# A hybrid encoder layer on one core: the first norm and the five begun weight pairs written out in a fixed order, TensorE kept turning the identity while it waits for x, the set-up vectors loaded later, and a weight pair begun after each tile of the two later norms

## The chip, the cores and the metric

The kernel runs on one core of one Trainium2 chip. The metric is the device time of one execution in microseconds (us). All times in this document are of that kind unless a sentence says otherwise. The engines carry the names of the profile: PE is TensorE's matrix multiplication and PEld its weight load, DVE is VectorE, ACT is ScalarE, POOL is GpSimd, SP is SyncE. ACTq, SPq and POOLq are the same engines where they issue a DMA transfer. "L113" is line 113 of the kernel before; the changed kernel has numbers of its own from its line 343 on.

## What is computed

One layer on x of 1024 rows by 1024 columns, all in float32:

```
x = x + 0.5 * swiglu_ffn(rms_norm(x, ffn1_norm), ffn1_w_in, ffn1_w_out)
u = rms_norm(x, mix_norm)
q_a,k_a,v_a, q_b,k_b,v_b, gate_logits = split(u @ w_mix_in)
y_a = chunked_band_attention(q_a, k_a, v_a, rel_bias_a)
lam = exp(sum(lambda_q1*lambda_k1)) - exp(sum(lambda_q2*lambda_k2)) + 0.2
y_b = rms_norm(diff_attention(q_b, k_b, v_b, t5_bias, lam), subln_g) * 0.8
g_a, g_b = split(sigmoid(gate_logits + b_gate))
x = x + (g_a*(y_a @ w_branch_a) + g_b*(y_b @ w_branch_b)) @ w_o
x = x + 0.5 * swiglu_ffn(rms_norm(x, ffn2_norm), ffn2_w_in, ffn2_w_out)
out = rms_norm(x, final_norm)
```

`swiglu_ffn` multiplies by a 1024 x 5632 matrix, takes silu(gate) * up and multiplies by a 2816 x 1024 matrix. Three small inputs return below as "the set-up vectors": the four lambda vectors of 64 numbers, `subln_g` of 128 and `b_gate` of 2048.

## The kernel before, in words

**A product in three pieces.** Every large float32 multiplication is made of three single-pass ones. Each operand is split into a high part, which an ACT cast rounds off (`whi` of a weight, `A11h` and the like of an activation, L97), and a low part, which DVE subtracts (`wlo`, `A11l`, L102). Then PE adds hi·hi, lo·hi and hi·lo (`mm3`, L128 to L130). "A product" below is one such PE instruction of 128x512.

**A pair in seven.** The multiplications by `ffn1_w_in` are made in Strassen-Winograd form. A pair is one block of 128 gate columns and the block of 128 up columns that goes with it. It needs seven block products, A11·B11, S1·T1, A12·B21, S2·T2, S4·B22, S3·T3 and A22·N4, of 12 PE products each. A11, A12, A22 and the sums S1 to S4 come from the normed and transposed x, and the B's and their differences T1 to T3 and N4 from the raw weights, which arrive in two transfers of 512 KB. PSUM has six banks for products ("mm") and two for transposes ("tr"). A pair holds three of the six in turn (its chains q, r and s). ACT copies a finished chain to SBUF (`c<-prod`, L287) or DVE adds the next one to it (`c<-prod,c`, L113), and only then is the bank free again.

**Begun pairs.** A11·B11 and A12·B21 need only the upper four row tiles and the first weight block. So five pairs are begun early (`head`, L343 to L348): these two block products are made, their sum is passed through silu and stored to a DRAM buffer (`gb`), and the other five are made later (`rest`, L350). The mixer's input projection begins seven pairs in the same way.

**Norms.** x has eight row tiles of 128. Each tile is loaded (`xt`), squared and summed on ACT (`junk`, L174), given its inverse root on POOL (`r<-v`, L139), scaled by DVE (L181) and transposed by PE in two halves of four (`tr`, L208). `norm0` (L214) makes A11 and A12 from tiles 0 to 3, `norm1a` S1 from tiles 4 to 7, `norm1b` S2 and S4, and `norm1c` S3 and A22. The opening (L657 to L688) does this for the first norm and calls the begun pairs between. `renorm` (L545) does it for the two later norms, behind `ffn1_w_out` (the mixer's norm) and behind `w_o`. There the rows are called `xc`, and `late` (L564) runs norm1a for its four tiles and then begins the remaining pairs by L571: `for _ in range(4 + extra_heads): next(projection, None)`.

**Set-up.** `setup` (L601) is a generator with four stages. Its first stage loads the set-up vectors on POOL's queue (`lv` L614, `gsub` L620, `bg_rows` L623), takes the dot products of the lambdas on DVE (L617) and transposes the gate bias (`trb`, L625). The later stages write the two relative-bias tables to DRAM. `ffn_in` calls it at pairs 5, 8, 11 and 14, each time behind the latest silu (`issue_after`). The exponentials of the two dot products (`le`, L776 and L777) stand in the text where attention begins.

**What sets the order.** Each engine runs its instructions in one fixed order, and an instruction that waits holds all behind it on its engine. A scheduler of the framework orders the program when it is built. It places each instruction by its own estimates of time, so that an instruction may run far from where its line stands. The names in the listings below have a number behind them that tells one buffer from the next.

## Time and profile before

| what | value |
|---|---|
| time, median of 3 runs | 2115.16 us (2114.83 to 2117.82) |
| time of the profiled execution | 2114.65 us |
| its span on the chip | 2112.9 us |
| mean granted TensorE clock | 0.993 |
| PE busy | 2045.6 us, 97% of the span, 9901 instructions |
| DVE busy | 1379.1 us, 65% |
| ACT busy | 955.5 us, 45% |
| POOL busy | 142.8 us, 7% |

The times of the views below are microseconds from the start of the span. The time of an execution is 1.75 us more than its span here (2114.65 less 2112.9). In a timeline a row reads: start, duration, engine, line, operation, output<-inputs, how many, and in brackets how long the engine was idle before it and what ended that. A row for several instructions runs to the end of the last. The end of a matmul in the trace is modelled, so the step from one start to the next is what tells its price.

### The profile page before, as it was taken

To read this page: it belongs to the slowest core of one execution; us is meant where nothing else is said; L and a number is where in the kernel's file an instruction comes from. 1 tells how busy PE (TensorE), PEld (TensorE's weight loads), DVE (VectorE), ACT (ScalarE), POOL (GpSimd) and SP (SyncE) were. 2 spreads that over 40 slices of the span, in tenths; PEclk is the share of its full clock that TensorE was granted. 3 is DMA by queue.
4 is the path that set the end of the run, shared out by engine and by line. 5 is a ranking of instruction groups with operands and counts; after the bars stand their busy time and mean duration, and the time that the engine had idled before them with its cause. 6 is when DMAs were issued, how large, how long until landed. Compare 5 with 4: busy or idle time off the path is not lost.

```text
span 2112.9 us, 28240 instructions
## 1 busy us (share of the span) xinstructions
PE 2045.6 (97%) x9901; PEld 1700.4 (80%) x9901; DVE 1379.1 (65%) x2459; ACT 955.5 (45%) x1825; POOL 142.8 (7%) x202
## 2 busy tenths in 40 slices
PE   6899999999999999999999999999899999999997
PEld 4688888888888788899877888787788888888886
DVE  6765656658567856654657787668766666668566
ACT  6433333334446644433467666157433333334444
POOL 2300000000001000000046211000000000000001
PEclk9999999999999999999999999999999999999999
DMA  5743323376344644743495365644542333275334
GB/s 166 213 135 100 125 86 104 105 261 214 99 135 143 195 135 130 234 145 115 158 302 178 111 221 167 229 139 127 163 144 91 125 96 107 92 278 201 99 116 160
DMA packets 272996, 324.61 MB, mean 154 GB/s; under 512 B 15070, under 2 KB 167662, under 8 KB 272852
## 3 DMA queue, kind: packets, MB, share of 16 engines
q1 hardware_dynamic: 271664, 319.55, 46.2%
q0 software_dynamic: 1184, 3.24, 0.6%
q8 instruction: 78, 1.28, 0.2%
q14 instruction: 66, 0.54, 0.1%
q10 hardware_dynamic: 4, 0.00, 0.0%
HBM read 221.74 MB, written 100.99 MB: 153 GB/s over the span
## 4 chain that ended last, share of the span: by engine, by line
PE 86%; DVE 6%; issue 3%; ACT 2%; DMA 2%; POOL 0%; SPq 0%; ACTq 0%; DVEq 0%; POOLq 0%
PE prod L128 19%; PE prod L129 19%; PE prod L130 18%; PE po L129 7%; PE po L128 7%; PE po L130 7%; PE pt L822 2%; DVE wlo L102 2%; PE pv L906 1%; PE pb L128 1%; PE pb L129 1%; PE pb L130 1%; PE sc L806 1%; PE sc L807 1%; PE pv L970 1%
## 5 line engine op out<-in xcount | busy, mean ns | idle before, releaser
L129 PE MATMUL po<-wlo,whi 128*128 128x512 f32 x744 | 291.1, 391 | 1.9 <-DVE wlo L102 1.8
L130 PE MATMUL po<-whi,wlo 128*128 128x512 f32 x744 | 289.6, 389 | 0.0
L97 ACT CAST whi<-raw 128x512 fp32r<-128x512 f32 x200 | 124.1, 622 | 294.3 <-PE prod L129 224.4
L97 ACT CAST whi<-T 128x512 fp32r<-128x512 f32 x192 | 119.1, 622 | 260.5 <-PE prod L129 248.0
L97 ACT CAST whi<-B 128x512 fp32r<-128x512 f32 x186 | 115.8, 622 | 262.1 <-PE po L129 255.0
L113 DVE TENSOR_TENSOR c<-prod,c 128x512 f32<-128x512 f32 x190 | 130.9, 690 | 146.1 <-PE prod L130 130.0
L102 DVE TENSOR_TENSOR wlo<-B,whi 128x512 fp32r<-128x512 f32 x186 | 128.1, 689 | 139.4 <-ACT whi L97 139.4
L102 DVE TENSOR_TENSOR wlo<-T,whi 128x512 fp32r<-128x512 f32 x192 | 131.8, 688 | 116.0 <-ACT whi L97 104.6
L128 PE MATMUL po<-whi 128*128 128x512 f32 x744 | 201.2, 390 | 0.0
L102 DVE TENSOR_TENSOR wlo<-raw,whi 128x512 fp32r<-128x512 f32 x200 | 137.3, 688 | 92.5 <-ACT whi L97 59.4
L129 PEld LDWEIGHTS po<-wlo,whi 128*128 128x128 f32 x744 | 139.6, 188 | 33.3 <-DVE wlo L102 4.6
L128 PEld LDWEIGHTS po<-whi 128*128 128x128 f32 x744 | 139.4, 188 | 29.0 <-ACT whi L97 0.2
L130 PEld LDWEIGHTS po<-whi,wlo 128*128 128x128 f32 x744 | 139.8, 188 | 28.4
L139 POOL TENSOR_TENSOR r<-v,neg_half 128x1 f32<-128x1 f32 x32 | 29.0, 913 | 1362.9 <-DVE v L180 1288.3
L102 DVE TENSOR_TENSOR wlo<-N,whi 128x512 fp32r<-128x512 f32 x64 | 44.1, 690 | 108.4 <-PE prod L129 69.0
L102 DVE TENSOR_TENSOR wlo<-ha,whi 128x512 fp32r<-128x512 f32 x154 | 105.5, 685 | 9.3 <-ACT whi L97 9.3
L287 ACT COPY c<-prod 128x512 f32<-128x512 f32 x186 | 102.1, 585 | 17.2 <-issue 10.5
L128 PE MATMUL prod<-A11h,whi 128*128 128x512 f32 x240 | 96.4, 402 | 7.9 <-DVE c L113 6.7
L816 ACT ACTIVATE pm<-pm,mn 128x640 f32<-128x640 f32 (+7 forms) x128 | 93.9, 735 | 19.7 <-DVE mn L814 17.0
L97 ACT CAST whi<-ha 128x512 fp32r<-128x512 f32 x154 | 94.8, 615 | 16.9 <-PE prod L129 11.4
L128 PE MATMUL prod<-A12h,whi 128*128 128x512 f32 x240 | 94.7, 394 | 3.4 <-DVE c L113 3.4
L814 DVE CUSTOM_DVE_ANT_0 pm<-sc,nb 128x640 f32<-128x640 f32 (+7 forms) x128 | 87.6, 701 | 14.7 <-PE sc L807 9.8
(236 smaller groups left out, 5018.8 us busy)
## 6 DMA issues: line engine op xcount, KB each, us to landing
raw<-in_ffn_w_in_dram SPq DMA_DIRECT2D x98, 512.0 KB, 4.2
raw<-in_w_mix_in_dram SPq DMA_DIRECT2D x47, 512.0 KB, 4.7
ha<-hS SPq DMA_DIRECT2D x88, 256.0 KB, 2.6
hA<-c SPq DMA_DIRECT2D x66, 256.0 KB, 4.1
ha<-hA SPq DMA_DIRECT2D x66, 256.0 KB, 2.7
B<-in_ffn_w_out_dram SPq DMA_DIRECT2D x12, 1024.0 KB, 11.7
hS<-hs SPq DMA_DIRECT2D x44, 256.0 KB, 2.4
hS<-c SPq DMA_DIRECT2D x44, 256.0 KB, 4.2
```

Of the source, the lines that this page charges most:

```text
L97: nc.scalar.copy(out=hi, in_=src)
L102: (nc.gpsimd if on_pool else nc.vector).tensor_tensor(out=lo, in0=src, in1=h, op=ALU.subtract)
L113: nc.vector.tensor_tensor(out=out_, in0=a, in1=b, op=op)
L128: nc.tensor.matmul(ps, a[0], b[0], start=first, stop=False, skip_group_check=shared)
L129: nc.tensor.matmul(ps, a[0], b[1], start=False, stop=False, skip_group_check=shared)
L130: nc.tensor.matmul(ps, a[1], b[0], start=False, stop=last, skip_group_check=shared)
L139: nc.gpsimd.tensor_tensor(out=r, in0=v, in1=neg_half, op=ALU.pow)
L287: nc.scalar.copy(out=self.held[name], in_=p)
L806: nc.tensor.matmul(sc[:, m, :wc], qs[:, h, c], ks[:, h, kc], start=True, stop=False)
L814: nc.vector.tensor_tensor_reduce(out=d3, in0=sc, in1=nb.rearrange("p (n w) -> p n w", n=n), scale=1.0, scalar=3e38, op0=ALU.add, op1=ALU.m ...
L816: nc.scalar.activation(out=dst, in_=dst, func=AF.Exp, bias=mn, scale=-1.0, accum_out=rs)
L822: nc.tensor.transpose(pt[:, b, :], p, ident)
```

## The change

**The opening.** The engines' orders are no longer left to the scheduler there but are those of the text (`tc.manual_schedule` on ACT, DVE, PE, POOL and SP). The rows 0 to 3 of x are issued in turn on SP's and ACT's queue, then come two weight blocks, then rows 4 to 7. The gain arrives as two rows of 512 in one transfer and is spread over the partitions by two matmuls with a column of the identity (`pg`); DVE copies it, a half at a time, where ACT did. Scaling goes by halves for the first four rows. `keep_busy` puts 48 transposes of the identity into a buffer that nobody reads (`pad`): 10 ahead of `pg`, 8 behind it, and six at a time between the transposes of x. The block products of the begun pairs are called one by one among the norm's steps.

**The set-up vectors.** Their transfers go to ACT's queue and are called at pair 5, behind its silu. What uses them (dots, gsub, trb) is called at pair 8, with the first table.

**The later norms.** `late` begins one pair after each of the tiles 1 to 3 and `1 + extra_heads` pairs behind the loop. The count is the same as before.

```diff
+        def open(self):
+            self.raw, self.ops = self.load(0), {}
+        def hi(self, m):
+            src = self.raw[:, :4] if m == 0 else self.raw[:, 4:]
+            self.ops[m] = [unit([P, 4, P], n) for n in ("whi", "wlo")]
+            nc.scalar.copy(out=self.ops[m][0], in_=src)
+        def multiply(self, m, k0=0, k1=4):
+            acc, _ = self.sums.acc(m)
+            w, a = self.ops[m], self.u[PRODUCTS[m][0]]
+            for k in range(k0, k1):
+                mm3(acc, [v[:, k, :] for v in w], [v[:, k, :] for v in a], k == 0, k == 3)
+        def taken(self, m):
+            self.sums.after(m, self.acc[m])
+            self.todo.remove(m)
...
@@ late
                 norm1a(t, row0[t], row1[t], u, ps)
-            for _ in range(4 + extra_heads):
+                if t:
+                    next(projection, None)
+            for _ in range(1 + extra_heads):
                 next(projection, None)
@@ setup
+        rows_ = []
         for q, k in ((lambda_q1, lambda_k1), (lambda_q2, lambda_k2)):
-            qk = []
             for v in (q, k):
-                vt = small.tile([P, B_DIM], F32, tag="lv", bufs=2, name="lv")
-                nc.gpsimd.dma_start(out=vt, in_=v[0].partition_broadcast(P))
-                qk.append(vt)
+                vt = small.tile([P, B_DIM], F32, tag="lv", bufs=4, name="lv")
+                nc.scalar.dma_start(out=vt, in_=v[0].partition_broadcast(P))
+                rows_.append(vt)
+        nc.scalar.dma_start(out=gsub, in_=subln_g[0].rearrange("(p o) -> p o", o=1))
+        bg_rows = wtemp([16, P], "bg_rows")
+        nc.scalar.dma_start(out=bg_rows, in_=b_gate[0].rearrange("(j p) -> j p", p=P))
+        yield
+        for q, k in (rows_[:2], rows_[2:]):
             dot = small.tile([P, 1], F32, tag="dot", name="dot")
...
-        nc.gpsimd.dma_start(out=gsub, in_=subln_g[0].rearrange("(p o) -> p o", o=1))
-        bg_rows = stage([16, P], "bg_rows")
-        nc.gpsimd.dma_start(out=bg_rows, in_=b_gate[0].rearrange("(j p) -> j p", p=P))
...
-        yield
         ea = stage([P, EA], "ea")
@@ opening
+        with tc.manual_schedule(engines={ACT, DVE, PE, Pool, SP}):
+            for t in range(4):
+                open_row(t, (nc.sync, nc.scalar)[t % 2])
+            for p in pairs[:2]:
+                p.open()
+            for t in range(4, 8):
+                open_row(t)
+            def keep_busy(n):
+                for k in range(n):
+                    nc.tensor.transpose(pad[:, k % 4, :], ident, ident)
+            keep_busy(10)
+            pg = []
+            for n in range(2):
+                pg.append(ps.tile([P, HALF], F32, tag="mm", bufs=6, name="pg"))
+                nc.tensor.matmul(pg[n], ident[:2, n:n + 1].to_broadcast([2, P]), g_row, start=True, stop=True)
+            keep_busy(8)
+            row[0].take()
+            root(0)
+            nc.vector.tensor_copy(out=gain[:, left], in_=pg[0])
+            row[1].take()
+            scaled(0, left)
+            turned_by(0, 0)
+            keep_busy(6)
...
+            p2.open()
+            p2.hi(0)
...
+            p3.multiply(2)
+            p4.open()
+            p4.hi(0)
+            p4.lo(0)
+            p3.taken(0)
+            p4.multiply(0)
+            p4.hi(2)
+            p4.lo(2)
+            p3.taken(2)
+            second(0)
+            second(1)
+            p4.multiply(2)
+            p4.taken(0)
+            second(2)
+            p4.taken(2)
+            second(3)
```

**Where instructions stand, first place: PE at the start.** Of the kernel before, the first rows of PE's order; `xt` is a row tile of x, `prod` a product bank:

```order
L667 MATMUL pg_252<-g_row_250,ones_247 128x512
L667 MATMUL pg_257<-g_row_255,ones_247 128x512
L208 MATMUL tr_269<-ident_66,xt_260 128x128 x4
L208 MATMUL tr_277<-ident_66,xt_260 128x128 x4
L208 MATMUL tr_294<-ident_66,xt_285 128x128 x4
L208 MATMUL tr_302<-ident_66,xt_285 128x128 x4
L208 MATMUL tr_319<-ident_66,xt_310 128x128 x4
L208 MATMUL tr_327<-ident_66,xt_310 128x128 x4
L208 MATMUL tr_344<-ident_66,xt_335 128x128 x4
L128 MATMUL prod_371<-A11h_233,whi_367 128x512
```

Of the changed kernel, the same stretch:

```order
L761 MATMUL pad_285<-ident_66 128x128 x10
L767 MATMUL pg_296<-g_row_255,ident_66 128x512
L767 MATMUL pg_298<-g_row_255,ident_66 128x512
L761 MATMUL pad_285<-ident_66 128x128 x8
L718 MATMUL tr_316<-ident_66,xt_257 128x128 x4
L761 MATMUL pad_285<-ident_66 128x128 x6
L718 MATMUL tr_334<-ident_66,xt_260 128x128 x4
L761 MATMUL pad_285<-ident_66 128x128 x6
L718 MATMUL tr_352<-ident_66,xt_257 128x128 x4
L761 MATMUL pad_285<-ident_66 128x128 x6
L718 MATMUL tr_365<-ident_66,xt_263 128x128 x4
L761 MATMUL pad_285<-ident_66 128x128 x6
```

Four more rows (a transpose of xt_260, six of the pad, a transpose of xt_266) stand ahead of the first product, `prod_410`. The left halves of the four rows are now turned first, with the pads between them, where both halves of each row were.

**Second place: DVE, where the begun pairs end and at the norm behind w_o.** Of the changed kernel, the rows from the last split of the fifth begun pair (`wlo_697`) to the addition that frees the s bank of the fourth (`c11_722`); `raw_764` and `raw_766` are the two weight blocks of pair 0, which is finished next:

```order
L113 TENSOR_TENSOR T1_768<-raw_766,raw_764 128x512
L113 TENSOR_TENSOR T2_789<-raw_766,T1_768 128x512
L113 TENSOR_TENSOR T3_828<-raw_766 128x512
L102 TENSOR_TENSOR S2l_240<-xt_260,S2h_239 128x4x128
L113 TENSOR_TENSOR xt_263<-s1_621,xt_263 128x512
L102 TENSOR_TENSOR wlo_771<-T1_768,whi_770 128x512
L102 TENSOR_TENSOR wlo_792<-T2_789,whi_791 128x512
L102 TENSOR_TENSOR wlo_810<-raw_766,whi_809 128x512
L102 TENSOR_TENSOR wlo_831<-T3_828,whi_830 128x512
L102 TENSOR_TENSOR S2l_240<-xt_263,S2h_239 128x4x128
L113 TENSOR_TENSOR c11_722<-prod_709,c11_722 128x512
```

The scheduler, which takes over behind the hand-written part, has put seven rows of pair 0 (T1 to T3 and four `wlo`), which need `raw_766`, ahead of `c11_722`, which belongs to the begun pairs.

Further on in DVE's order, at the norm behind w_o, the sum of the second tile (`s1`) and the first addition that frees a begun pair's bank (`c11`). Of the kernel before, the last rows ahead of that addition; the second tile's `s1_13807` stands 20 rows ahead of it, and the sums of the third and fourth tile (`s1_13831`, `s1_13855`) stand between:

```order
L113 TENSOR_TENSOR T2_14141<-raw_14118,T1_14120 128x512
L113 TENSOR_TENSOR T3_14180<-raw_14118 128x512
L102 TENSOR_TENSOR wlo_14123<-T1_14120,whi_14122 128x512
L113 TENSOR_TENSOR s1_13855<-tr_13850,xc_13484 128x512
L113 TENSOR_TENSOR xc_13484<-xt_13303,tr_13850 128x512
L102 TENSOR_TENSOR A22l_14097<-xc_13484,A22h_14096 128x4x128
L113 TENSOR_TENSOR c11_13884<-prod_13890,c11_13884 128x512
```

Of the changed kernel, from the second tile's sum on:

```order
L113 TENSOR_TENSOR s1_13859<-tr_13854,xc_13532 128x512
L113 TENSOR_TENSOR xc_13532<-xt_13349,tr_13854 128x512
L102 TENSOR_TENSOR A22l_14149<-xc_13530,A22h_14148 128x4x128
L102 TENSOR_TENSOR A22l_14149<-xc_13532,A22h_14148 128x4x128
L102 TENSOR_TENSOR wlo_14127<-raw_14105,whi_14126 128x512
L113 TENSOR_TENSOR xt_13349<-s1_13859,xt_13349 128x512
L113 TENSOR_TENSOR c11_13888<-prod_13894,c11_13888 128x512
```

The addition now stands six rows behind the second tile's sum, ahead of the third and fourth tile's.

**Third place: ACT at the set-up vectors.** Of the kernel before, ACT's rows around the silu of pair 3 (`gate_1169`); the transfers of `lv` are on POOL's queue here, and the first `le` is ACT's seventh row (`L776 ACTIVATE le_9310<-dot_1245 128x1`):

```order
L97 CAST whi_1264<-raw_1260 128x512
L97 CAST whi_1285<-N4_1283 128x512
L97 CAST whi_1306<-T1_1304 128x512
L97 CAST whi_1325<-raw_1260 128x512
L401 ACTIVATE gate_1169<-prod_594 128x512
L97 CAST whi_1346<-T2_1344 128x512
L97 CAST whi_1364<-raw_1262 128x512
L287 COPY c12_1201<-prod_659 128x512
```

Of the changed kernel, the same silu (`gate_1221`) and what follows; ahead of it stands one cast of pair 5, `whi_1308`:

```order
L425 ACTIVATE gate_1221<-prod_636 128x512
L643 DMA lv_1293<-in_lambda_q1_dram 128x64
L643 DMA lv_1295<-in_lambda_k1_dram 128x64
L643 DMA lv_1297<-in_lambda_q2_dram 128x64
L643 DMA lv_1299<-in_lambda_k2_dram 128x64
L287 COPY c12_1253<-prod_683 128x512
L645 DMA gsub_227<-in_subln_g_dram 128x1
L647 DMA bg_rows_1302<-in_b_gate_dram 16x128
L287 COPY c11_1325<-prod_1312 128x512
L993 ACT_TABLE_LOAD
L993 ACTIVATE le_9362<-dot_1741 128x1
L97 CAST whi_1329<-N4_1327 128x512
```

The scheduler has put six transfer issues and the exponential of the first dot product among the casts, and the casts of N4 and T1 of pair 5 behind them, which before stood ahead of the silu.

More of the change, by code (lines that the diff above doesn't have):

```diff
@@ L341, in load, with lo @@
             return load(w_cols(self.w, self.c[n], P), raw_tile([P, KT, P]))
+        def open(self):
[4 more added lines that the diff above has]
+            nc.scalar.copy(out=self.ops[m][0], in_=src)
+        def lo(self, m):
+            src = self.raw[:, :4] if m == 0 else self.raw[:, 4:]
+            add(self.ops[m][1], src, self.ops[m][0].bitcast(F32), ALU.subtract)
+        def multiply(self, m, k0=0, k1=4):
[3 more added lines that the diff above has]
+                mm3(acc, [v[:, k, :] for v in w], [v[:, k, :] for v in a], k == 0, k == 3)
+            self.acc = getattr(self, "acc", {})
+            self.acc[m] = acc
+        def taken(self, m):
+            self.sums.after(m, self.acc[m])
+            self.todo.remove(m)
         def head(self):
@@ L362, in run_all, with ffn_in @@
             pass
-    def ffn_in(w_in, u, ps, extra=None):
+    def ffn_in(w_in, u, ps, extra=None, opened=None):
         silu, hid = [], {}
@@ L413, in ffn_in @@
         pairs = [Pair(w_in, j * P, FF + j * P, u, ps, make_sink(j)) for j in range(NF)]
-        for p in pairs[:HEADS]:
+        if opened is not None:
+            opened += pairs[:HEADS]
+            yield
+        for p in pairs[:HEADS] if opened is None else ():
             p.head()
@@ L607, in negate @@
             nc.gpsimd.tensor_scalar(out=dst, in0=src, scalar1=-1.0, scalar2=None, op0=ALU.mult)
+        rows_ = []
         for q, k in ((lambda_q1, lambda_k1), (lambda_q2, lambda_k2)):
-            qk = []
             for v in (q, k):
-                vt = small.tile([P, B_DIM], F32, tag="lv", bufs=2, name="lv")
-                nc.gpsimd.dma_start(out=vt, in_=v[0].partition_broadcast(P))
-                qk.append(vt)
+                vt = small.tile([P, B_DIM], F32, tag="lv", bufs=4, name="lv")
[4 more added lines that the diff above has]
+        nc.scalar.dma_start(out=bg_rows, in_=b_gate[0].rearrange("(j p) -> j p", p=P))
+        yield
+        for q, k in (rows_[:2], rows_[2:]):
             dot = small.tile([P, 1], F32, tag="dot", name="dot")
-            nc.vector.tensor_tensor_reduce(out=qk[0], in0=qk[0], in1=qk[1], scale=1.0, scalar=0.0,
+            nc.vector.tensor_tensor_reduce(out=q, in0=q, in1=k, scale=1.0, scalar=0.0,
                                            op0=ALU.mult, op1=ALU.add, accum_out=dot)
             lams.append(dot)
-        nc.gpsimd.dma_start(out=gsub, in_=subln_g[0].rearrange("(p o) -> p o", o=1))
         nc.gpsimd.tensor_scalar(out=gsub, in0=gsub, scalar1=1.0 - LAMBDA_INIT, scalar2=None, op0=ALU.mult)
-        bg_rows = stage([16, P], "bg_rows")
-        nc.gpsimd.dma_start(out=bg_rows, in_=b_gate[0].rearrange("(j p) -> j p", p=P))
         trb = ps.tile([P, 4, P], F32, tag="tr", bufs=2, name="trb")
@@ L659, in hybrid_layer_kernel @@
         u = new_u(U_OPS)
-        ones = const.tile([1, P], F32, name="ones")
-        nc.vector.memset(ones, 1.0)
-        gain = sb.tile([P, D], F32, tag="gain", bufs=1, name="gain")
-        for part in range(2):
-            g_row = wtemp([1, HALF], "g_row")
-            nc.scalar.dma_start(out=g_row, in_=ffn1_norm[0][part * HALF:(part + 1) * HALF].rearrange("(o d) -> o d", o=1))
-            pg = ps.tile([P, HALF], F32, tag="mm", bufs=6, name="pg")
-            nc.tensor.matmul(pg, ones, g_row, start=True, stop=True)
-            nc.scalar.copy(out=halves(gain)[part], in_=pg)
@@ L669, in hybrid_layer_kernel @@
-        ffn1 = ffn_in(ffn1_w_in[0], u, ps, setup(ps))
-        row0, row1 = [], []
-        for t in range(4):
-            row0.append(Row(load(rows(x)[t], raw_tile([P, D], "xt"))))
-            row0[t].take()
-            row0[t].scale(gain)
-            norm0(t, row0[t], u, ps)
-        next(ffn1, None)
-        for t in range(4):
-            row1.append(Row(load(rows(x)[4 + t], raw_tile([P, D], "xt"))))
-            row1[t].take()
-            row1[t].scale(gain)
-            norm1a(t, row0[t], row1[t], u, ps)
@@ L687, in hybrid_layer_kernel @@
+        row0, row1 = row[:4], row[4:]
         for t in range(4):
```

164 lines of the change are left out of this document (159 added, 5 removed).

## The prediction, made before the changed kernel was run

> **What bounds the kernel now.** I read the page's shares first, then the chain of waits.
>
> ```profile
> span 2112.9 us, 28240 instructions
> PE 2045.6 (97%) x9901; PEld 1700.4 (80%) x9901; DVE 1379.1 (65%) x2459; ACT 955.5 (45%) x1825; POOL 142.8 (7%) x202
> PE 86%; DVE 6%; issue 3%; ACT 2%; DMA 2%; POOL 0%; SPq 0%; ACTq 0%; DVEq 0%; POOLq 0%
> ```
>
> PE sets the time. It does the same products before and after, so only its idle time and the time at the lower clock can change. The next rows are windows: stretch, length, PE busy (instructions), PEld, DVE, ACT, POOL, granted clock, DMA share, GB/s. They cover the opening, a stretch of steady work, the mixer's norm and the norm behind w_o.
>
> ```profile
> 0.00:100.00 100.00, 73.29 (x301) 56.18 (x302) 67.59 (x115) 56.06 (x101) 32.27 (x60) 0.97 0.63 187
> 100.00:200.00 100.00, 100.00 (x443) 82.82 (x442) 63.86 (x100) 35.58 (x63) 0.00 (x0) 1.00 0.41 130
> 690.00:740.00 50.00, 46.71 (x211) 37.57 (x209) 41.60 (x68) 32.97 (x58) 0.00 (x0) 0.97 0.66 192
> 1470.00:1510.00 40.00, 30.24 (x126) 23.67 (x125) 32.66 (x54) 22.50 (x40) 0.00 (x0) 0.87 0.66 191
> ```
>
> In steady work a product costs 100/443 = 0.226 us and nothing is lost. Of the 301 instructions of the first 100 us, 64 are transposes of x and 5 others are small, which leaves 232 products, worth 52.4 us. So the opening loses 47.6 us by 100 us. The places to work on are the opening, the set-up in the steady stretch, and the two later norms.
>
> **The opening up to the end of the begun pairs.** PE's timeline:
>
> ```profile
> 3.27 3.75 PE L667 MATMUL pg<-g_row,ones 1*128 1x512 f32 x4 [3.27 <-DMA g_row<-in_ffn_norm_dram]
> 12.85 1.97 PE L208 MATMUL tr<-ident,xt 128*128 128x128 f32 x8 [5.84 <-DVE xt L181]
> 30.61 0.79 PE L128 MATMUL prod<-A11h,whi 128*128 128x512 f32 x1 [0.67 <-ACT A11h L97]
> 46.74 1.03 PE L208 MATMUL tr<-ident,xt 128*128 128x128 f32 x8
> 61.48 0.79 PE L128 MATMUL prod<-A12h,whi 128*128 128x512 f32 x1 [3.37 <-DVE c L113]
> ```
>
> The first transpose comes at 12.85 and the first product at 30.61. The chain of waits and POOL say why the first is so late:
>
> ```profile
> 1.99 7.31 DMA lv<-in_lambda_k_dram
> 9.71 0.20 ACT L776 ACTIVATE le<-dot 128x1 f32<-128x1 f32 x1 [2.21 <-DVE dot L617]
> 5.90 0.56 POOL L139 TENSOR_TENSOR r<-v,neg_half 128x1 f32<-128x1 f32 x1 [1.73 <-DVE v L180]
> 15.33 1.54 POOL L139 TENSOR_TENSOR r<-v,neg_half 128x1 f32<-128x1 f32 x1 [1.25 <-DVE v L180]
> ```
>
> ACT held the second gain half behind the `le` that waits for the lambda transfer. Both are gone from here. Placed by hand, each row starting when its engine is free and its inputs are there: ten pads at 0.25 us from about 2.5 (cold spacing: 1.97/8), `pg` to about 9, in its shadow row 0's squares (1.06) and root (0.56), a gain half on DVE (0.60), the scaling (0.60), the first transpose at 9 to 10. From there to the first product DVE has twelve steps of 0.60 and ACT four casts and two squares between PE's turns: 17 us, 13.6 earlier than now. The pads wait for nothing but the identity, and by then PE waits for rows, so the other 38 pads at 1.03/8 = 0.13 cost nothing.
>
> From 17 on PE is fed by arrivals, not by order. The 120 products of the five begun pairs (27.1 us) and ten more groups of four transposes (5) would end at 49. The later rows of x and the weights, 512 KB each, arrive more slowly than that:
>
> ```profile
> xt<-in_x_dram SPq DMA_DIRECT2D x8, 512.0 KB, 8.9
> raw<-in_ffn_w_in_dram SPq DMA_DIRECT2D x12, 512.0 KB, 4.2
> ```
>
> and the fifth pair's load stands on SP's queue behind the store of the third pair's silu, at about 47. It lands 4.2 later, and its block products end at about 59.5. So by 59.5 the new order has done 120 products and lost 59.5 - 27.1 = 32.4. The old one at 60 us had lost 39.9 (89 products). The lead is 7 us.
>
> **Where the lead goes.** Pair 0 comes next. The second weight block of it, `raw_766`, takes the buffer of the fifth pair's block, so its load is issued at 54, after `wlo_697`, and lands at 58.2. The listing of DVE has eleven rows from T1 to `c11_722`, and PE's S1·T1 writes the bank that `c11_722` frees.
>
> ```profile
> 55.34 0.69 DVE L113 TENSOR_TENSOR T<-raw,T 128x512 f32<-128x512 f32 x1
> 55.95 0.69 DVE L113 TENSOR_TENSOR T<-raw 128x512 f32<-128x512 f32 x1
> ```
>
> Such rows step by 0.60, so 58.2 + 11 x 0.60 = 64.8, and PE stands from 59.5 to about 65: 5.5. Smaller waits follow for S2, S3 and T2, 4.2 us in my placing, and the clock falls twice. What a fall costs, from two rows of the opening and one window (columns as above):
>
> ```profile
> 33.34 0.63 PE L129 MATMUL prod<-A11l,whi 128*128 128x512 f32 x1
> 33.77 0.63 PE L130 MATMUL prod<-A11h,wlo 128*128 128x512 f32 x1
> 1483.36:1488.64 5.28, 5.28 (x12) 4.13 (x13) 5.28 (x10) 3.06 (x6) 0.00 (x0) 0.50 0.45 140
> ```
>
> A product at the low clock steps by 0.43, so it loses 0.2 against 0.226. Behind the w_o norm twelve products ran so, which is 2.4; the estimate for a fall here is 2. Sum 32.4 + 5.5 + 4.2 + 2 x 2 = 46.1, and up to 48 where POOL's root takes 1.54 and not 0.56 at each of the first rows. Against 47.6 now I take **0** (-6.5 if the wait for `c11_722` is hidden, +3 if roots and arrivals all come late).
>
> **Do pads hold the clock?** A window in the attention whose PE work is mostly transposes (whole kernel, and of the transposes' line L822 alone), the next one, and one that let it fall:
>
> ```profile
> 1116.66:1120.07 3.41, 2.66 (x22) 2.05 (x20) 2.55 (x7) 2.87 (x8) 3.10 (x3) 1.00 0.55 173
> 1116.66:1120.07 3.41, 2.33 (x16) 1.68 (x16) 1.00 0.55 173
> 1120.07:1123.48 3.41, 3.41 (x34) 2.42 (x32) 0.23 (x1) 0.96 (x2) 1.25 (x1) 1.00 1.01 414
> 1314.64:1318.05 3.41, 1.39 (x6) 1.02 (x7) 0.48 (x1) 0.47 (x1) 0.81 (x2) 1.00 0.95 334
> 1318.05:1321.46 3.41, 3.41 (x10) 2.63 (x9) 0.00 (x0) 0.00 (x0) 0.00 (x0) 0.50 0.46 177
> ```
>
> With 16 transposes among 22 instructions the clock stayed 1.00 afterwards; with 1.39 us busy it fell to 0.50. So I count transposes as work. If they didn't count, PE would be cold to about 21, over some 35 pads and turns that stand in its way and 24 products: 35 x 0.12 = 4 and 24 x 0.2 = 5, **+9** together.
>
> The Trainium skill, "TensorE: Matmul & The Clock Gate", Part 4 (PE-mode transpose), states that full clock doesn't engage in transpose mode. By that rule the pads would buy nothing, and the sum would be the +9 case. The rows above speak against it.
>
> **The set-up vectors.** Before, PE loses nothing there (100.00 busy). After, ACT's row `gate_1221` waits some 10 us for the last block product of pair 3 with a single cast ahead of it, and behind it everything that PE needs next is queued. Prices:
>
> ```profile
> 0.73 0.77 ACTq L665 DMA_DIRECT2D g_row<-in_ffn_norm_dram  x2
> 56.05 1.55 ACT L287 COPY c<-prod 128x512 f32<-128x512 f32 x3
> 40.96 1.28 ACT L401 ACT_TABLE_LOAD   x1
> 46.96 1.14 ACT L97 CAST A22h<-xt 128x512 fp32r<-128x512 f32 x2
> bg_rows<-in_b_gate_dram POOLq DMA_DIRECT2D x1, 8.0 KB, 2.2
> lv<-in_lambda_k_dram POOLq DMA_DIRECT2D x2, 32.0 KB, 6.2
> ```
>
> An issue is 0.39, a copy 0.48 (1.55 for three, the last with its tail), a cast 0.52. First, PE's S3·T3 of pair 4 overwrites the bank that `c12_1253` copies: silu 0.48, four issues 1.6, copy 0.48, less the last product that PE has meanwhile: PE stands 2.7. Then gsub and bg_rows 0.8, a copy 0.48, the table 1.28, `le` after the dot after the lambda's landing, then the casts of N4 and T1 (0.52 each) and a `wlo` (0.60): 5.5 or more on ACT against 2.7 of products on PE, which stands about 3 before S1·T1 of pair 5, and 1.2 at the transpose of bg_rows, which needs its landing. With a fall of the clock (2): **+9**. If a landing takes 6.2 as in the crowded opening, +13; if PE has other work at both places, +2.
>
> **The later norms.**
>
> ```profile
> 700.63 0.66 PE L208 MATMUL tr<-ident,xc 128*128 128x128 f32 x4 [0.55 <-ACT xc L225]
> 702.29 0.66 PE L208 MATMUL tr<-ident,xc 128*128 128x128 f32 x4 [1.00 <-ACT xc L225]
> 703.42 0.63 PE L128 MATMUL prod<-A11h,whi 128*128 128x512 f32 x1 [0.48 <-ACT p L287]
> 1473.79 0.66 PE L208 MATMUL tr<-ident,xc 128*128 128x128 f32 x4 [0.24 <-ACT xc L225]
> 1476.00 0.66 PE L208 MATMUL tr<-ident,xc 128*128 128x128 f32 x4 [1.56 <-ACT xc L225]
> 1483.36 0.79 PE L128 MATMUL prod<-A11h,whi 128*128 128x512 f32 x1 [6.70 <-DVE c L113]
> ```
>
> Behind w_o, PE stands 8.5 and then makes the twelve cold products, 2.4 more: 10.9. The 6.70 is the wait for the first `c<-prod,c` of a begun pair, which frees a bank. By the listing of DVE it stands 20 rows behind the sum of the second tile before and six rows now: 14 x 0.60 = 8.4 earlier, so this bank no longer decides. The scalings and transposes of the third and fourth tile then do: 0.4, 0.5, 2.7 and 0.8 in my placing, and a fall of the clock: 6.4. Difference **-4.5** (0 if the stop only moves, -8 if there is no fall and half the waits).
>
> In the mixer's norm 0.55 + 1.00 + 0.48 are lost and a fall. In the new order one wait of 3.2 for DVE stands ahead of a begun pair, with the same fall: **+1.5** (0 to +3.5).
>
> **Sum.** 0 + 9 + 1.5 - 4.5 = +6 on the profiled execution's 2114.65, 2120.7. The median of the runs is 0.5 above that execution: **2121**. What a measurement here can tell from no change begins at 0.2%, 4.2 us: faster is under 2111, slower over 2119.4.
>
> **Rivals.** A, the forecast: 0.47. B, the set-up stop stays hidden: if PE's order has pair 5's A11·B11 and pair 4's blocks in stock when ACT returns, the 2.7 and 3 shrink under 1, and some of the lead of 7 us at 59.5 survives because the bank wait is shorter than eleven rows: -3 + 1 + 1.5 - 4.5 = -5, 2110. It decides once `c11_722` or S1·T1 comes 3 us sooner than I place it. For it: PE at 100.00 in 100 to 200 and DVE only 64% busy there. Against: one FIFO on ACT, with a wait at its head. 0.18. C, the terms cancel: set-up +4 (one stop only), the rest as above: +1, 2116. 0.20. D, transposes don't count for the clock: +6 + 9, 2130. 0.10. E, the lambdas take 6.2 to land at pair 5 too: +13 - 3 = +10, 2125. 0.05.
>
> The range of 8 in 10 is 2110 to 2131, from B's centre to D's; A's own is 2117 to 2126. Faster by over 0.2%: most of B and a tail of C, 0.18. Slower: some four fifths of A, with D and E, 0.53. Same: the rest of the three, 0.29.
>
> **What would show it.** Right: the first product of PE at 16 to 18; a wait of 5 to 6 near 60 to 65 that ends with DVE's `c`; PE under 100 in 130 to 160, with ACT's `lv` issues, the table load and `le` beside it; the 6.70 of w_o down to 3 or less. Granted clock near 1 from about 9 on would bear the pads out, 0.5 to 20 would be D. Wrong: PE full from 130 to 160 (B), or no wait at 60 to 65.

## The result, and the profile after

The changed kernel takes 2132.07 us (median of 4 runs, 2128.09 to 2133.23), the kernel before 2115.96 beside it (4 runs, 2114.83 to 2117.82). The ratio is 1.0071, with a 95% interval of 1.0055 to 1.0087. It is slower, by 15 us by the ratio and by 16.1 between the medians, where the forecast was 6. The time lies about 1 us above the upper end of the forecast range, 2131.

The page of the changed kernel:

```profile
span 2129.1 us, 28332 instructions
PE 2061.4 (97%) x9949; PEld 1711.2 (80%) x9949; DVE 1379.1 (65%) x2464; ACT 958.2 (45%) x1825; POOL 140.2 (7%) x196
```

PE still bounds it, and its span is 16.2 us longer. Windows of the changed kernel (columns as in the prediction) show how much of that came by 100 us and by 200 us:

```profile
0.00:100.00 100.00, 76.42 (x320) 58.27 (x320) 66.47 (x109) 52.05 (x93) 27.27 (x53) 0.91 0.58 172
100.00:200.00 100.00, 95.86 (x413) 77.83 (x414) 61.23 (x102) 35.47 (x61) 0.55 (x1) 0.98 0.45 140
```

Of the 320 PE instructions of the first 100 us, 48 are pads, 4 belong to the gain and 64 are transposes of x. That leaves 204 products where the kernel before had 232: 28 x 0.226 = 6.3 us behind. From 100 to 200 it makes 413 where the kernel before made 443: 30 x 0.226 = 6.8 us. All experiments below are counted so.

Farther on the same DVE rows can be matched by name and order in the two traces. The median shift of the matched rows, after less before:

| stretch (time in the kernel before) | shift at its end | of it here | forecast |
|---|---|---|---|
| opening and set-up, to the end of the first FFN | +13.0 | +13.0 (6.3 + 6.8 by the counts) | 0 + 9 |
| mixer's norm | +15.7 | +2.7 | +1.5 |
| attention, most of it at 1240 | +20.2 | +4.5 | none |
| norm behind w_o | +15.3 | -4.9 | -4.5 |
| end of the span | +16.2 | +0.9 | none |

PE's timeline of the changed kernel holds the places, in order: the opening, the end of the begun pairs, the set-up, and the two norms.

```profile
2.67 2.40 PE L761 MATMUL pad<-ident 128*128 128x128 f32 x10 [2.67 <-POOL ident masks.py:199]
8.71 1.97 PE L761 MATMUL pad<-ident 128*128 128x128 f32 x8
18.85 0.50 PE L128 MATMUL prod<-A11h,whi 128*128 128x512 f32 x1 [0.68 <-ACT A11h L724]
59.94 0.79 PE L128 MATMUL prod<-A11h,whi 128*128 128x512 f32 x1 [6.69 <-ACT whi L349]
73.48 0.77 PE L128 MATMUL prod<-S1h,whi 128*128 128x512 f32 x1 [5.34 <-DVE c L113]
148.95 0.50 PE L128 MATMUL prod<-S3h,whi 128*128 128x512 f32 x1 [2.35 <-ACT c L287]
155.18 0.51 PE L128 MATMUL prod<-S1h,whi 128*128 128x512 f32 x1 [1.70 <-ACT whi L97]
729.30 0.80 PE L128 MATMUL prod<-A11h,whi 128*128 128x512 f32 x1 [4.10 <-DVE c L113]
1501.33 0.50 PE L128 MATMUL prod<-A12h,whi 128*128 128x512 f32 x1 [2.48 <-DVE c L113]
```

The first product comes 11.8 us sooner (18.85 against 30.61; 16 to 18 was forecast), and from the third on the products step by 0.23, which is the full clock. The wait for `c` at the end of the begun pairs is there (5.34), and so are the two waits at the set-up and the shortened one behind w_o (2.48 where 6.70 stood). The wait of 6.69 at 59.94 was not in the sum. It is for the fifth begun pair's weights. The DMA issues on SP's queue, the bias table's on POOL's, and ACT's first use of the weights say why:

```profile
48.73 1.30 POOL L667 DMA_DIRECT2D diag_a<-ea  x2 [0.30 <-POOL ea L673]
49.53 12.48 SPq L119 DMA_DIRECT2D raw<-in_ffn_w_in_dram  x3
59.27 0.62 ACT L349 CAST whi<-raw 128x512 fp32r<-128x512 f32 x1 [9.00 <-DMA raw<-in_ffn_w_in_dram]
```

The load is the first of the three issues. It is issued at 49.53 and is there at 59.27, 9.7 us later, where such loads take 4.2. Two writes of the bias table, 384 KB each, were issued 0.8 us ahead of it. In the kernel before they came 15 us later, since POOL's queue stood behind PE's transpose of the gate bias:

```profile
58.42 0.64 POOL L641 DMA_DIRECT2D ea<-in_rel_bias_a_dram  x1 [30.99 <-PE trb L625]
63.99 1.28 POOL L636 DMA_DIRECT2D diag_a<-ea  x2 [0.30 <-POOL ea L643]
```

Ahead of the experiments the theory was this. T: the early table writes slow that load and cost the opening its lead, and ACT's queue stops PE at the set-up. Its first rival, Q: the load is late by its place on SP's queue.

### The profile page after: what moved, and what is told of

Read it like the earlier page. It is cut to its first block, busy times and chain, and to the rows that moved or that the text cites. A ratio compares the mean times of both kernels' runs of the same rounds, so it can differ in the third digit from the quotient of the medians.

```text
span 2129.1 us, 28332 instructions
## 1 busy us (share of the span) xinstructions
PE 2061.4 (97%) x9949; PEld 1711.2 (80%) x9949; DVE 1379.1 (65%) x2464; ACT 958.2 (45%) x1825; POOL 140.2 (7%) x196
## 4 chain that ended last, share of the span: by engine, by line
PE 86%; DVE 6%; DMA 3%; issue 2%; ACT 2%; POOL 0%; ACTq 0%; SPq 0%; DVEq 0%; POOLq 0%
PE prod L128 18%; PE prod L129 18%; PE prod L130 18%; PE po L129 7%; PE po L130 7%; PE po L128 7%; PE pt L1039 2%; PE pv L1123 1%; PE pb L128 1%; PE pb L129 1%; DVE wlo L102 1%; DMA raw<-in_ffn_w_in_dram 1%; PE sc L1023 1%; PE pb L130 1%; PE sc L1024 1%
## 5 line engine op out<-in xcount | busy, mean ns | idle before, releaser
L97 ACT CAST whi<-raw 128x512 fp32r<-128x512 f32 x190 | 118.1, 622 | 286.3 <-PE prod L129 229.0
L102 DVE TENSOR_TENSOR wlo<-raw,whi 128x512 fp32r<-128x512 f32 x190 | 130.7, 688 | 113.0 <-ACT whi L97 59.6
L287 ACT COPY c<-prod 128x512 f32<-128x512 f32 x186 | 104.0, 583 | 19.1 <-issue 10.1
L1033 ACT ACTIVATE pm<-pm,mn 128x640 f32<-128x640 f32 (+7 forms) x128 | 93.9, 734 | 22.2 <-DVE mn L1031 19.5
L128 PE MATMUL prod<-S1h,whi 128*128 128x512 f32 x240 | 94.9, 395 | 8.6 <-DVE c L113 6.9
L97 ACT CAST whi<-ha 128x512 fp32r<-128x512 f32 x154 | 94.8, 616 | 18.2 <-PE prod L129 11.9
```

The lines of the kernel that those rows point to most:

```text
L97: nc.scalar.copy(out=hi, in_=src)
L102: (nc.gpsimd if on_pool else nc.vector).tensor_tensor(out=lo, in0=src, in1=h, op=ALU.subtract)
L128: nc.tensor.matmul(ps, a[0], b[0], start=first, stop=False, skip_group_check=shared)
L287: nc.scalar.copy(out=self.held[name], in_=p)
L1033: nc.scalar.activation(out=dst, in_=dst, func=AF.Exp, bias=mn, scale=-1.0, accum_out=rs)
```

## The experiments

### e1: the bias tables late again

```diff
-        bg_rows = wtemp([16, P], "bg_rows")
+        bg_rows = stage([16, P], "bg_rows")
```

> The changed kernel with one word changed: the buffer of the gate-bias rows is again the one that the bias table is built in, so the table's load and its two writes of 384 KB wait until the gate bias has been transposed, near 150 us, as they waited for it near 58 us in the kernel before. Theory T (the opening lost its lead because those writes, begun at 48.7, slowed the fifth begun pair's weight load, issued at 49.5, from about 4.2 to 9.7 us): the load lands in 4 to 5 us, PE's wait of 6.69 at 59.94 shrinks to 1 to 2, and PE is some 5 us ahead by 100 us. The scheduler also moves the casts of N4 and T1 of pair 5 ahead of the silu here, so the set-up stop should shrink by 2 to 4 more. Time 2120 to 2127. Rival Q (the load is late by its place on SP's queue behind the third pair's store, whatever else is moving): the load still takes 8 to 10 us, the wait stays at 6 to 7, time 2128 to 2133 but for the set-up's 2 to 4.

Measured: 2123.97 us, ratio 1.0035 (1.0022 to 1.0048). Windows of e1:

```profile
0.00:100.00 100.00, 78.52 (x348) 60.55 (x349) 68.84 (x113) 53.89 (x96) 6.02 (x15) 0.95 0.57 166
100.00:200.00 100.00, 98.37 (x433) 80.81 (x432) 64.29 (x104) 38.02 (x66) 20.17 (x39) 1.00 0.48 147
```

ACT's first use of the fifth pair's weights in e1 and PE's next long wait, from the timeline:

```profile
53.97 0.62 ACT L349 CAST whi<-raw 128x512 fp32r<-128x512 f32 x1 [4.36 <-DMA raw<-in_ffn_w_in_dram]
67.28 0.76 PE L128 MATMUL prod<-S1h,whi 128*128 128x512 f32 x1 [6.62 <-DVE c L113]
```

With the tables out of the way the load, issued at 48.87, is there at 53.97, 5.1 us later. By 100 us PE has 348 - 116 = 232 products (116 are the pads, the gain's four and the transposes), as many as the kernel before: the whole 6.3 us are back, and T holds for the opening. The set-up costs 10 x 0.226 = 2.3 and not 6.8. Three more casts now stand ahead of the silu, and ACT waits 2.10 there and not 10.26; that this is the reason is likely, but no run has it alone. The changed opening is worth nothing by 100 us even so. PE waits until 67.28 for the bank.

### e2: the set-up as before, the rest as changed

```diff
-                nc.scalar.dma_start(out=vt, in_=v[0].partition_broadcast(P))
+                nc.gpsimd.dma_start(out=vt, in_=v[0].partition_broadcast(P))
...
-        bg_rows = wtemp([16, P], "bg_rows")
-        nc.scalar.dma_start(out=bg_rows, in_=b_gate[0].rearrange("(j p) -> j p", p=P))
-        yield
...
+        bg_rows = stage([16, P], "bg_rows")
+        nc.gpsimd.dma_start(out=bg_rows, in_=b_gate[0].rearrange("(j p) -> j p", p=P))
...
+        yield
         ea = stage([P, EA], "ea")
```

> The changed kernel with the set-up as it was: vectors on POOL's queue at the start, their exponentials in the opening. Theory T: no stop between 140 and 160 (7 us back), the table writes wait for the gate bias's transpose again and leave the fifth pair's load alone (5 back), and the opening pays up to 2 for DVE's wait for the lambdas ahead of the first scaling: 2119 to 2124. Rival S (the stop near 150 comes from the order of the casts around the silu, not from the set-up): PE still stands 4 us or more there, 2124 to 2128.

Measured: 2123.59 us, ratio 1.0028 (1.0017 to 1.0040). Windows of e2:

```profile
0.00:100.00 100.00, 77.97 (x339) 59.16 (x340) 68.58 (x119) 54.24 (x98) 34.44 (x60) 0.95 0.65 187
100.00:200.00 100.00, 100.00 (x443) 82.78 (x442) 63.94 (x101) 35.55 (x62) 0.00 (x0) 1.00 0.40 127
```

Nothing is lost from 100 to 200, so the stop was the set-up's. The opening pays 2.3 (339 less 116 and the bias transpose is 222 products, ten short), most of it since DVE waits for the lambdas ahead of the first gain copy: the first product comes at 19.98, 1.8 later than in e1.

### e7: the new set-up alone

The kernel before with the diff of `setup` and, for the room, this:

```diff
-        ones = const.tile([1, P], F32, name="ones")
-        nc.vector.memset(ones, 1.0)
...
-            nc.tensor.matmul(pg, ones, g_row, start=True, stop=True)
+            nc.tensor.matmul(pg, ident[:1, :1].to_broadcast([1, P]), g_row, start=True, stop=True)
```

> The kernel before with the new set-up alone (vectors on ACT's queue behind pair 5's silu, the gate-bias rows in a buffer of their own); the row of ones that spreads the gain is the identity's corner here, to make room. Theory: ACT's queue stops PE between 140 and 170 us for 2 to 7 us, and the lambda transfer no longer holds the opening (1 to 3 back): 2115 to 2122. Rival (the stop needs the hand-written opening ahead of it): PE stays full from 100 to 200 us, 2112 to 2115.

Measured: 2122.92 us, a little above the 2115 to 2122 expected, ratio 1.0022 (1.0013 to 1.0032). Windows of e7:

```profile
0.00:100.00 100.00, 75.46 (x308) 58.14 (x309) 67.89 (x110) 56.70 (x100) 30.01 (x53) 0.97 0.64 193
100.00:200.00 100.00, 94.19 (x409) 77.17 (x408) 60.55 (x101) 35.97 (x61) 0.45 (x1) 0.98 0.37 119
```

The set-up costs 34 x 0.226 = 7.7 us between 100 and 200 with no hand-written opening ahead of it. It gives 1.8 back in the opening: 308 less 68 is 240 products, 8 more. The rival falls. ACT's timeline of the changed kernel shows the queue:

```profile
146.42 0.60 ACT L425 ACTIVATE gate<-prod 128x512 f32<-128x512 f32 x1 [10.26 <-PE prod L130]
146.43 0.34 ACTq L643 DMA_DIRECT2D lv<-in_lambda_q_dram  x1
148.32 0.58 ACT L287 COPY c<-prod 128x512 f32<-128x512 f32 x1 [1.30 <-DVE c L433]
150.53 1.28 ACT L993 ACT_TABLE_LOAD   x1
154.51 0.62 ACT L97 CAST whi<-T 128x512 fp32r<-128x512 f32 x1 [1.23 <-DVE T L113]
```

ACT sits 10.26 us at the silu. The copy that PE's S3·T3 waits for comes 1.9 us after it, and the cast that S1·T1 waits for 8.1 after it.

### e3: the later norms alone

```diff
                 norm1a(t, row0[t], row1[t], u, ps)
-            for _ in range(4 + extra_heads):
+                if t:
+                    next(projection, None)
+            for _ in range(1 + extra_heads):
```

> The kernel before with the pairs of the two later norms begun one per tile, and nothing else. From the shift of the same DVE rows between the two traces: +2.7 in the mixer's norm and -4.9 behind w_o, together -2: 2113 to 2115 where before is 2116. Rival (the two differ because of what stood ahead of them): the two shifts come out otherwise, 2112 to 2119.

Measured: 2115.69 us, ratio 0.9997 (0.9988 to 1.0006): no difference that can be measured. By matched rows the mixer's norm costs 1.7 and the one behind w_o gives 4.4, as forecast in sign and nearly in size. Between them the attention shifts by 4.2 here too, though nothing in it was changed.

### e0: the kernel before once more

> The kernel before, unchanged, for a second profiled execution. In all five other traces the same DVE rows of the attention come 3.3 to 3.9 us later from 1240 us of the kernel before on, at a wait for a bias tile. If that is a matter of the execution and not of the changes, this trace may show it too, and differs from the first by less than 0.5 us everywhere else; if it belongs to the changes, this trace lacks it.

Measured: 2117.10 us. Up to 1240 its rows lie within 0.6 us of the first execution's, and then shift by 3.0. PE's wait at that place in the first execution of the kernel before:

```profile
1242.07 0.39 PE L806 MATMUL sc<-ks,qs 128*128 128x256 f32 x1 [0.94 <-DVE mn L814]
```

In the second:

```profile
1242.82 0.39 PE L806 MATMUL sc<-ks,qs 128*128 128x256 f32 x1 [1.97 <-DVE mn L814]
```

In the changed kernel, with DVE's wait ahead of it:

```profile
1259.90 0.29 DVE L1031 CUSTOM_DVE_ANT_0 pm<-sc,nb 128x128 f32<-128x128 f32 x1 [5.17 <-DMA nb<-diag_b]
1260.25 0.58 PE L1023 MATMUL sc<-ks,qs 128*128 128x256 f32 x1 [3.08 <-DVE mn L1031]
```

A bias tile (`nb`) lands later or earlier from one execution to the next: DVE's wait for it is 3.05 in the first execution of the kernel before and 4.07 in the second. In the second the clock falls right behind it (0.50 in this window, where the first execution's stayed at 1.00):

```profile
1245.55:1248.96 3.41, 3.41 (x18) 3.41 (x17) 2.18 (x9) 1.63 (x7) 0.00 (x0) 0.50 0.23 82
```

The first profiled execution of the kernel before was a lucky one there. So about 3 of the 16.2 us between the two profiles can come without any part of the change. The medians, 16.1 apart, average over such luck and are what the result rests on; how the attention's part is spread over the runs that left no trace stays open.

### e4: 40 of the 48 pads left out

```diff
-                for k in range(n):
+                for k in range(n if n == 8 else 0):
                     nc.tensor.transpose(pad[:, k % 4, :], ident, ident)
```

> The changed kernel with 40 of the 48 pads left out (the 8 behind the gain's matmuls stay). Theory P (transposes raise and hold the clock): the first product comes 1 to 3 us sooner, since PE is busy without a gap from 5 to 18 us and 24 pads lie on that stretch, but products run at 0.43 for one to two clock windows: +1 to +4 at 30 us, of which the later waits for weights take most, so 2131 to 2135. Rival (transposes don't count for the clock): the clock at the first product is the same with and without pads, and leaving them out only gains: 2128 to 2131.

Measured: 2130.46 us (2127.46 to 2133.16), ratio 1.0071 (1.0054 to 1.0088), the same as with pads as far as this tells. From the timeline of e4, PE's first products, and farther on the issues and the use of the fifth pair's weights:

```profile
16.07 0.50 PE L128 MATMUL prod<-A11h,whi 128*128 128x512 f32 x1 [0.68 <-ACT A11h L724]
17.14 0.39 PE L130 MATMUL prod<-A11h,wlo 128*128 128x512 f32 x1
17.37 0.39 PE L128 MATMUL prod<-A11h,whi 128*128 128x512 f32 x1
```

```profile
46.73 7.04 SPq L119 DMA_DIRECT2D raw<-in_ffn_w_in_dram  x3
46.98 1.30 POOL L667 DMA_DIRECT2D diag_a<-ea  x2 [0.30 <-POOL ea L673]
51.02 0.62 ACT L349 CAST whi<-raw 128x512 fp32r<-128x512 f32 x1 [3.55 <-DMA raw<-in_ffn_w_in_dram]
```

The first 100 us of this execution:

```profile
0.00:100.00 100.00, 76.22 (x308) 56.49 (x309) 69.21 (x113) 54.03 (x96) 28.05 (x53) 0.93 0.64 187
```

The first product comes 2.8 us sooner without the 40 pads, and the products are at the full clock at once (0.23 from 17.14 to 17.37), so the 8 pads left, the transposes of x and the gain's matmuls had raised it by themselves. Both theories missed in this execution: P had expected products at 0.43, and the rival that transposes don't count. They count. The load was issued at 46.73, ahead of the table's writes, took 4.3 us, and by 100 us PE was level with the kernel before (308 less 8 pads and 68 is 232 products). A second execution of each kernel tells how much of this repeats.

### a_again and e4_again: who is first

> The changed kernel, unchanged, for a second profiled execution. In the first the table's two writes were issued at 48.73, 0.80 us ahead of the fifth pair's load (49.53), which took 9.7 us. Theory T: who is first is set by the order of the work, so the load again takes 8 to 10 us and PE waits 6 to 7 for it; 2128 to 2133. Rival (chance of one execution): the load takes 4 to 5.

> e4 (40 of the 48 pads left out) for a second profiled execution. In its first the load was issued at 46.73, 0.25 us ahead of the table's writes (46.98), and took 4.3 us; that execution was the fastest of its four (2127.5, the others 2129.7 to 2133.2). Theory T2 (the load is slow only when the writes get in ahead of it): if the writes come first here, the load takes 8 to 10 us, if the load is first, 4 to 5. Rival: the load's time does not follow who is first.

Measured: 2133.23 and 2126.23 us. Neither changes its kernel. The second execution of the changed kernel, with the writes 0.80 ahead:

```profile
48.13 1.31 POOL L667 DMA_DIRECT2D diag_a<-ea  x2 [0.30 <-POOL ea L673]
48.93 2.73 SPq L119 DMA_DIRECT2D raw<-in_ffn_w_in_dram  x2
59.09 0.62 ACT L349 CAST whi<-raw 128x512 fp32r<-128x512 f32 x1 [9.42 <-DMA raw<-in_ffn_w_in_dram]
```

The second of e4, with the load 0.26 ahead:

```profile
48.53 7.21 SPq L119 DMA_DIRECT2D raw<-in_ffn_w_in_dram  x3
48.79 1.30 POOL L667 DMA_DIRECT2D diag_a<-ea  x2 [0.30 <-POOL ea L673]
52.99 0.62 ACT L349 CAST whi<-raw 128x512 fp32r<-128x512 f32 x1 [3.72 <-DMA raw<-in_ffn_w_in_dram]
```

In four executions the load took 9.7 and 10.2 us with the writes 0.8 us ahead of it, and 4.3 and 4.5 us with the writes 0.25 us behind it. The order goes with the kernel here: no execution of e4 had the writes first, and none of the changed kernel the load. But e4 has the other case too. Its next weight load, issued at 47.21, 0.23 us behind the first write, landed 10.1 us later (11.8 in the second execution), and the same load in e1, without writes, 6.2 us later. So what follows the writes is late, as T2 says. That the other runs of e4 were slower because the writes came first there is possible, but they left no trace.

The clock did not repeat. PE's first products in the second execution of e4, and its first 100 us:

```profile
17.77 0.79 PE L128 MATMUL prod<-A11h,whi 128*128 128x512 f32 x1 [0.68 <-ACT A11h L724]
19.09 0.63 PE L130 MATMUL prod<-A11h,wlo 128*128 128x512 f32 x1
19.51 0.63 PE L128 MATMUL prod<-A11h,whi 128*128 128x512 f32 x1
```

```profile
0.00:100.00 100.00, 74.21 (x297) 55.06 (x298) 67.64 (x111) 53.92 (x96) 28.07 (x53) 0.93 0.65 186
```

Here the first six products run at the low clock (0.42 from 19.09 to 19.51), as P had it, and by 100 us PE has 221 products, 11 fewer than in the first execution. PE's longest gap among the transposes was 2.52 us in this execution and 1.48 in the first; that this made the difference is not shown. The changed kernel, with its pads, had the full clock at its first product in both of its executions (18.85 and 18.19), and so had b1 and b2 below, which leave the 40 pads out. So the pads are not always needed, but without them the full clock at the first product is not certain.

### e5 and e6: why the lead is gone even without the tables

Both stand on e1 (`stage` for the gate-bias rows). e5 takes the fifth pair's results ahead of the S2 rows:

```diff
-            second(0)
-            second(1)
             p4.multiply(2)
             p4.taken(0)
-            second(2)
             p4.taken(2)
-            second(3)
+            for t in range(4):
+                second(t)
```

> e1 with the fifth pair's results taken ahead of the S2 rows, so that on DVE the addition that frees the bank (c11) stands three rows behind T1 and not ten. In e1 PE stood 6.62 us, to 67.28, for that addition. Theory B (the bank alone holds PE there): S1 x T1 of pair 0 starts at 63 to 64 and PE has done 3 to 4 us more by 100 us, 2119 to 2122 beside e1's 2124. Theory W (DVE has too much left to do from 57 on, 28 rows of S2, S4, S3 and A22 beside pair 0's): the wait moves to S2 x T2, whose rows now come later; by 100 us less than 1 us is gained, 2123 to 2126.

e6 makes S2 right behind S1 and S3 and A22 behind the last S1:

```diff
                 nc.scalar.copy(out=s1h, in_=s1)
+                add(a11, s1, a11, ALU.subtract)
+                nc.scalar.copy(out=s2h, in_=a11)
                 add(s1l, s1, s1h.bitcast(F32), ALU.subtract)
...
             p3.multiply(2)
+            for t in range(4):
+                norm1c(t, row[4 + t], u)
```

> e1 with the 16 DVE rows that make S2, S3 and A22 (and their ACT casts) moved into the idle times that DVE has between 31 and 55 us, where the fixed order had put them behind the begun pairs. The scheduler then places T1 of the next pair too ahead of the addition that frees the bank (13 rows from T1 on). Theory W: PE has lost 43 to 46 by 100 us where e1 lost 48.5; 2118 to 2122. Theory B: the addition comes no sooner than in e1, PE stands until 67 or later, and nothing is gained: 2123 to 2127.

Measured: e5 2133.12 us, ratio 1.0070 (1.0055 to 1.0085); e6 2121.21 us, ratio 1.0018 (1.0008 to 1.0027). The first 100 us of e5:

```profile
0.00:100.00 100.00, 77.09 (x310) 57.88 (x311) 64.90 (x106) 51.38 (x91) 6.03 (x15) 0.90 0.55 160
```

PE's waits in e5's timeline:

```profile
64.24 0.47 PE L128 MATMUL prod<-S1h,whi 128*128 128x512 f32 x1 [2.53 <-ACT whi L97]
74.64 0.80 PE L128 MATMUL prod<-S2h,whi 128*128 128x512 f32 x1 [5.15 <-ACT S2h L97]
```

The first 100 us of e6:

```profile
0.00:100.00 100.00, 83.63 (x370) 65.29 (x371) 72.25 (x118) 55.42 (x99) 6.01 (x15) 0.95 0.57 174
```

In e5 S1·T1 does begin 3 us sooner than in e1 (64.24), and PE then waits 5.15 for S2, whose rows now come later. By 100 us it is 38 products, 8.6 us, worse than e1, more than W had said; the granted clock over the 100 us is 0.90 where e1's is 0.95. Freeing the bank alone gains nothing. In e6 PE has 370 - 116 = 254 products by 100 us, 22 more than the kernel before: 5.0 us gained. So what had eaten the lead is DVE's work, with the ACT casts that belong to it. The changed kernel's order has the 24 rows of S2, S4, S3 and A22 (the expectation says 28) at the end of the begun pairs and behind them, where DVE has no time to spare, and leaves DVE a third idle between 20 and 55: it is busy for 22.2 of these 35 us in e1 and for 28.7 in e6, which moves 16 of the 24 rows.

e6 is still 4 us slower than the kernel before. It pays 2.5 at the set-up (432 products from 100 to 200, 11 short), and by matched rows 6.0 in the mixer's norm, where the changed kernel pays 2.7. Why that norm costs more here is not settled.

### b1 and b2: what the runs point to

b1 is e6 without the 40 pads, with the lambdas on POOL's queue and their exponentials in the hand-written opening, only the gate-bias rows on ACT's queue, the mixer's norm as before and the one behind w_o as changed:

```diff
+            for v in (lambda_q1, lambda_k1, lambda_q2, lambda_k2):
+                vt = small.tile([P, B_DIM], F32, tag="lv", bufs=4, name="lv")
+                nc.gpsimd.dma_start(out=vt, in_=v[0].partition_broadcast(P))
...
             p0.taken(0)
+            nc.scalar.activation(out=e1, in_=lams[0], func=AF.Exp)
+            nc.scalar.activation(out=e2, in_=lams[1], func=AF.Exp)
...
-                if t:
+                if t and per_tile:
                     next(projection, None)
```

> All that the runs point to: the fixed order with the sums early (e6), the 40 pads left out (e4), the lambdas on POOL's queue and their exponentials in the opening by hand where no engine waits for them, only the gate-bias rows on ACT's queue behind pair 5's silu, the mixer's norm as in the kernel before and the norm behind w_o as changed. Theory: PE has lost 42 to 44 by 100 us (before 48.5), stays full from 100 to 200, shifts by under 1 in the mixer's norm and by -2 to -4.5 behind w_o: 2106 to 2111 where before is 2117. Rival (each part was measured beside others and the scheduler's order changes with every one): new stops eat it up, 2113 to 2120.

b2 also opens the weight blocks of the fourth and fifth begun pair sooner (the expectation counts from 0) and splits the S3 and A22 rows around the fifth pair:

```diff
             p2.open()
+            p3.open()
...
+            p4.open()
...
-            for t in range(4):
+            for t in range(2):
                 norm1c(t, row[4 + t], u)
             p4.hi(0)
```

> The same with the third and fourth weight block of the begun pairs loaded ahead of two stores on SP's queue, and half of the S3 and A22 rows behind the fifth pair's split, so that PE waits less for that pair (4.37 + 2.41 us in e6). Theory W: DVE's rows are only moved, and come back as waits at S1 and S2 of pairs 0 and 1: within 1 us of b1 by 100 us. Rival: the 4 to 5 us of those waits are gained: 2102 to 2107.

Measured: b1 2108.91 us (2105.16 to 2110.34), ratio 0.9963 (0.9951 to 0.9975); b2 2110.14 us, ratio 0.9972 (0.9960 to 0.9983). Windows of b1:

```profile
0.00:100.00 100.00, 80.72 (x333) 61.31 (x334) 73.45 (x125) 56.20 (x102) 9.03 (x21) 0.95 0.60 176
100.00:200.00 100.00, 100.00 (x443) 82.58 (x442) 65.06 (x101) 34.67 (x62) 19.17 (x38) 1.00 0.49 148
```

333 less 8 pads and 68 is 257 products by 100 us, 25 more than before: 5.6 us. Nothing is lost at the set-up, 0.5 in the mixer's norm, and 4.7 are gained behind w_o. b1 beats both kernels, the one before by 0.4%. It changes several things at once, so it does not tell what each is worth. b2 gains 1.1 more by 100 us (262 products), about as W had it, and no difference to b1 in the time is shown.

## Why the prediction was right or wrong

**The sign and the bound.** Right. PE bounds the kernel, makes the same products, and only its waits and its clock moved.

**The set-up.** The step was right in place, cause and nearly in size: ACT's silu with everything queued behind it, two waits and a fall of the clock, 6.8 to 7.9 in the changed kernel's two executions and 7.7 alone (e7), where 9 was forecast. The waits were 2.35 and 1.70, not 2.7, 3 and 1.2: the lambdas landed in 3 us, and PE did not wait for the gate-bias rows.

**The opening.** This is the step that failed: "It lands 4.2 later", for the fifth pair's load. The load took 9.7, and the opening came out at +6.3 where 0 was forecast, with bounds of -6.5 to +3. The prediction followed SP's queue and not POOL's. With the gate-bias rows in a buffer of their own nothing holds the table's load and writes any more: they came at 48.73, and with the old buffer back (e1) they were gone from the opening. Rival E had the slow landing at the wrong transfer.

**Where the lead goes.** The wait for `c11` came (5.34, forecast 5.5), and e1, with the load on time, is level with the kernel before at 100 us, as the sum had it. But the reason given, eleven rows ahead of one bank, was only the first of a chain. e5 freed that bank sooner and lost; e6 moved the work and gained.

**The pads.** That transposes hold the clock was right. In the changed kernel the step of the pads fell from 0.21 to 0.11 near 13.8, with nothing but transposes and the gain's four matmuls before it, and the first product found the full clock. The prediction had that clock from about 9 on. That the pads cost nothing was wrong: PE worked without a gap from 8.71 to the end of the last transpose at 18.2, and without 40 of them the first product came at 16.07 and 17.77, not at 18.85 and 18.19. Nor did they do nothing: without them the first six products ran at the low clock in one of e4's two executions. By 100 us e1, with the pads, and e4's first execution have 232 products each, so the later waits take the difference up. The Trainium skill, "TensorE: Matmul & The Clock Gate", Part 4 (PE-mode transpose), has it that the full clock doesn't engage in transpose mode. In the first execution of e4 PE had done nothing but the gain's four matmuls and 32 transposes (8 pads and 24 of x) between 2.66 and 15.4 us, and then its products ran at full clock. So this trace does not agree with the page, and rival D fell. That D's time, 2130, is nearest to the measured one is coincidence.

**The later norms.** -4.9 behind w_o (forecast -4.5) and +2.7 in the mixer's (+1.5): right in place and sign. e3 alone gives -4.4 and +1.7. The sizes are less firm than these two kernels make them look: by matched rows, the traces of the other kernels that begin a pair per tile read -1.5 to -4.7 behind w_o and +1.1 to +6.0 in the mixer's norm.

**The attention.** Not in the sum. Of the 4.5 us between the two profiles, 3.0 are shown to come without the change, from one execution to the next (e0); the rest is not settled.

**The rivals.** B's bet, that the stop at the set-up stays hidden, failed in every kernel with the new set-up, and C's single stop did not occur in the changed kernel either. With the measured sizes the sum is 6.3 + 6.8 + 2.7 - 4.9 + 4.5 + 0.9 = 16.3 on 2114.65: 2130.9. That this is the profiled execution's own time (2130.93) is no test, since the terms are read off the same two traces. Of the last two terms 3.0 can come with the execution.

## What to carry to other kernels

When an order is written out by hand, write the work of the second engine into the idle time of the first stretch too: a first product 12 us sooner was worth nothing while DVE's sums were left for the end. Giving a small tensor a buffer of its own can also remove the wait that kept a large, patient transfer out of the way, so follow every queue that the change frees, not only those that it names. Issues and table loads behind a waiting activation hold all its engine's casts; put them where the engine has casts in stock, or in the opening.
